# First keys and queries in fp32 through the sync queue, rounded on VectorE and ScalarE, in a hard-max attention kernel

## The chip, the cores and the metric

The kernel runs on one core of a Trainium2 chip. The metric is the device time of one execution in microseconds (us). The kernel before took 443.18 us (median of three runs, 442.71 to 443.21). The profile shown here is of one execution, whose span from first to last instruction is 441.9 us.

## The reference

For each of 4 batches there are 4096 queries and 4096 keys of 128 numbers. Each query gets the row of `v` that belongs to its best key:

```python
logits = np.matmul(q, k.transpose(0, 2, 1))      # 4 x 4096 x 4096
best = np.argmax(logits, axis=-1)
return v[b_idx, best, :]                          # 4 x 4096 x 128, fp32
```

## The kernel before

A tile is 128 queries; there are 32 tiles per batch and 128 in all. For each tile, TensorE (PE) screens all 4096 keys of the batch in fp16, not one by one but in groups of four. The transposed keys `kT` hold sums and differences of key pairs. `dpart` (line 228) multiplies a query tile with the differences, and ScalarE (ACT) takes the absolute value of the 1024 results into `A` (line 234). `spart` multiplies with the sums, and adds `A` on PE through an identity matrix. ACT turns one half into `E` (line 247), VectorE (DVE) takes the maximum of `E` and the other half into `W` (line 260, `fold`), and `max` reads the eight best groups of `W` (line 264, `top`). So a tile needs three ACT passes (two `A`, one `E`) and two long DVE passes, and PE keeps four PSUM buffers (pool `ps`, tag `u`) in turn.

Behind this screen, GpSimd (POOL) gathers the key group of each winner by indirect DMA (`kg`, line 282), DVE forms the fp16 dot products and picks one of four keys (lines 300 to 333), and POOL gathers the rows of `v` (`vr`, line 342), which SyncE (SP) writes out. Rows whose result is too close to call are collected twice, halfway and at the end, and are worked out again in fp32; the tiles `FQ`, `FK`, `FV` and `FR` belong to that, and are set to zero at the start.

All five engines are under a hand-written order: each engine executes its instructions in the order in which the program text issues them, and a queue (SP's and POOL's also) is held up by the first instruction that waits.

The change touches the start, before the first tile. There the order is this.

- Lines 105 and 106: POOL issues DMAs which read fp32 keys and queries of batch 0 and write them as fp16: the first half of the keys (`natk[0]`, half 0, 512 KB written) and query tiles 0 to 3 (`natq[0]`). After the identity matrix (lines 115 and 116) it issues the second half in two pieces, query tiles 4 to 7 and query tiles 8 to 31. Then come POOL's constants: three `W` iotas (line 131), small iotas, `ones`, `tri` (line 161), and the zero fills (lines 171 and 172). After these POOL issues the key loads of batch 1 (line 66).
- Lines 108 to 113: DVE clears `wz`, and PE runs 14 matmuls on it, into two of the four PSUM buffers.
- Lines 665 to 679: `trn_half(u, h, ms, put)` makes one quarter `u` of `kT` for key half `h`. Eight matmuls with an identity (or its negative, `identn`) transpose and add or subtract key pairs; a copy out of PSUM, by ACT (`by_act`, line 190) or DVE (`by_dve`, line 193), follows. Half 0 of the keys is done first, then query tiles 0 to 3 (`trn_q`, line 214), then half 1 in two steps, `ms` (0, 1) and (2, 3), one for each piece. Then the first `dpart` can run.
- `put_k` (line 75) subtracts keys within groups on DVE into `kd`, and SP stores them to DRAM for the later gathers (line 78). `turn_q` (line 208) has SP issue a DMA that transposes query tiles: tiles 4 to 7 first, then 8 to 15 and so on. Tile 4 needs the first of these. SP's order before is: store of `put_k(0, 0)`, transposes of tiles 4 to 7 and 8 to 15, store of `put_k(0, 1)`, two more transposes.

Of the kernel before, what the change touches and what calls it, by code (L numbers as in the profile page):

```python
# [7 lines left out]
FP32 = mybir.dt.float32  # L8
# [8 lines left out]
AF = mybir.ActivationFunctionType  # L17
# [12 lines left out]
def kernel(ctx, tc, q, k, v, out):  # L30
    nc = tc.nc
    B, Sq, D = q.shape
    Sk = k.shape[1]
    P = 128
    NQT = Sq // P
# [10 lines left out]
    bp = ctx.enter_context(tc.tile_pool(name="kq", bufs=1))  # L46
# [13 lines left out]
    natk = [bp.tile([P, 2, 16, P], FP16, name=f"natk{i}", tag=f"natk{i}") for i in range(2)]  # L60
    kd = bp.tile([P, 2, 4, 3, P], FP16, name="kd", tag="kd")
    natq = [bp.tile([P, NQT, P], FP16, name=f"natq{i}", tag=f"natq{i}") for i in range(2)]

    def load_k(b, h, x, y):
        kb = k[b].rearrange("(h p n) d -> p h n d", p=P, n=16)
        nc.gpsimd.dma_start(out=natk[b % 2][:, h, x:y], in_=kb[:, h, x:y])  # L66

    def load_q(b, x, y):
        nc.gpsimd.dma_start(out=natq[b % 2][:, x:y], in_=q[b].rearrange("(p t) d -> p t d", p=P)[:, x:y])  # L69

    def put_k(b, h):
        if b >= B:
            return
        src = natk[b % 2][:, h].rearrange("p (g f) d -> p g f d", f=4)
        nc.vector.tensor_tensor(out=kd[:, h], in0=src[:, :, 1:4, :], in1=src[:, :, 0:1, :].to_broadcast([P, 4, 3, P]),
                                op=OP.subtract)
        kb16 = k16[b].rearrange("(h p n) d -> p h (n d)", p=P, n=16)
        nc.sync.dma_start(out=kb16[:, h], in_=kd[:, h].rearrange("p g f d -> p (g f d)"))
# [23 lines left out]
        else:  # L102
            load_q(b, (i - 8) * NQT // 8, (i - 8 + n // 4) * NQT // 8)

    load_k(0, 0, 0, 16)
    load_q(0, 0, 4)

    wz = cp.tile([P, 512], FP16, tag="wz")
    nc.vector.memset(wz, 0.0)
# [4 lines left out]

    ident = cp.tile([P, P], FP32, tag="ident")
    masks.make_identity(nc, ident)
    load_k(0, 1, 0, 8)
    load_k(0, 1, 8, 16)
    load_q(0, 4, 8)
    load_q(0, 8, NQT)  # L120
    identh = cp.tile([P, P], FP16, tag="identh")
    nc.vector.tensor_copy(out=identh, in_=ident)
    identn = cp.tile([P, P], FP16, tag="identn")
# [6 lines left out]
    for W in W_t:  # L130
        nc.gpsimd.iota(out=W.bitcast(U16)[:, 0::2].rearrange("p (h m r) -> p h m r", h=2, m=4),
                       pattern=[[-NG * 2, 2], [-4, 4], [-16, P]], base=IDX, channel_multiplier=0)

    def iota(name, n, base, mult=0):
        x = cp.tile([P, n], FP32, name=name, tag=name)
        nc.gpsimd.iota(out=x, pattern=[[0 if mult else 1, n]], base=base, channel_multiplier=mult,
                       allow_small_or_imprecise_dtypes=True)
        return x
# [28 lines left out]
    FR = cp.tile([P, 8], U32, tag="FR")  # L167
    FQ = cp.tile([P, P], FP32, tag="FQ")
    FK = cp.tile([P, 3, 512], FP32, tag="FK")
    FV = cp.tile([P, P], FP32, tag="FV")  # L170
    for z in (FR, FQ, FK, FV):
        nc.gpsimd.memset(z, 0)

    tk_t = {}

    def trn_half(u, h, ms, put=None):
        x = 2 * (u // 2)
        if ms[0] == 0:
            tk_t[u] = pp.tile([P, 512], FP32, tag="u", name=f"tk_{u}_{h}")
        ps = tk_t[u]  # L180
        for m in ms:
            o = ps[:, m * P:(m + 1) * P]
            nc.tensor.matmul(out=o, lhsT=natk[0][:, h, 4 * m + x, :], rhs=identh, start=True, stop=False)
            nc.tensor.matmul(out=o, lhsT=natk[0][:, h, 4 * m + x + 1, :],
                             rhs=identn if u % 2 else identh, start=False, stop=True)
        if put is not None:
            put(kT[0][:, u * 1024 + h * 512:u * 1024 + h * 512 + 512], ps)

    def by_act(dst, src):
        nc.scalar.activation(out=dst, in_=src, func=AF.Copy)  # L190
# [20 lines left out]
    def trn_q(x, y, put):  # L211
        ps = pp.tile([P, 512], FP32, tag="u", name=f"tq_{x}")
        for i in range(x, y):
            nc.tensor.matmul(out=ps[:, (i - x) * P:(i - x + 1) * P], lhsT=natq[0][:, i, :], rhs=identh,
                             start=True, stop=True)
        put(qT[0][:, x * P:y * P], ps)
# [5 lines left out]
    def mm(ps, t, u, stop):  # L222
        b, qt = t // NQT, t % NQT
        for n in range(2):
            nc.tensor.matmul(out=ps[:, n * 512:(n + 1) * 512], lhsT=qT[b % 2][:, qt * P:(qt + 1) * P],  # L225
                             rhs=kT[b % 2][:, u * 1024 + n * 512:u * 1024 + (n + 1) * 512], start=True, stop=stop)

    def dpart(t, x):
        if t >= T:
            return  # L230
        ps = pp.tile([P, 1024], FP32, tag="u", name=f"pd_{t}_{x}")
        mm(ps, t, 1 + 2 * x, True)
        A = ep.tile([P, 1024], FP16, tag=f"A{x}", name=f"A_{t}_{x}")
        nc.scalar.activation(out=A, in_=ps, func=AF.Abs)  # L234
        A_t[t, x] = A
# [427 lines left out]
                nc.vector.tensor_scalar(out=base, in0=base, scalar1=float(Sk), scalar2=None, op0=OP.add)  # L663

    ALL = range(4)
    trn_half(1, 0, ALL, by_act)
    trn_half(3, 0, ALL, by_dve)
    trn_half(0, 0, ALL, by_act)
    trn_q(0, 4, by_dve)
    trn_half(2, 0, ALL, by_act)  # L670
    put_k(0, 0)
    for u in (1, 3, 0, 2):
        trn_half(u, 1, (0, 1))
    trn_half(1, 1, (2, 3), by_act)
# [2 lines left out]
    trn_half(2, 1, (2, 3), by_dve)  # L677
    dpart(0, 0)
    dpart(0, 1)
    nc.vector.tensor_copy(out=iota_h, in_=iota_r)  # L680
    nc.vector.tensor_copy(out=rec2[:, :, 1], in_=iota_p.to_broadcast([P, SLOTS]))
    cuts = list(range(0, 96 + 1, 8)) + list(range(96 + 4, T - 3, 4)) + [T - 2, T]
# [106 lines left out]
    for b in range(1, B):  # L789
        x = b * NQT  # L790
# [115 lines left out]
```

## Time and profile before

| engine | busy us | share of the span |
|---|---|---|
| DVE | 405.9 | 92% |
| PE | 378.9 | 86% |
| ACT | 375.6 | 85% |
| POOL | 306.2 | 69% |

A share of busy time is an average over the whole span. The stages differ:

| stage, us | ACT busy, us | DVE busy, us | POOL busy, us |
|---|---|---|---|
| 0 to 13 (loads, transposes of batch 0) | 3.71 | 4.11 | 11.78 |
| 13 to 40 (first tiles) | 27.00 | 20.26 | 8.53 |
| 40 to 110 | 70.00 | 69.28 | 43.50 |
| 110 to 220 | 109.54 | 110.00 | 81.68 |
| 220 to 330 | 101.33 | 109.72 | 83.03 |
| 330 to 425 | 64.03 | 90.90 | 69.71 |

The first stage is the only one before the tail in which neither ACT nor DVE is full.

### The profile page before, as it was taken

The numbers are of one execution on the slowest core, as the hardware profiler recorded it, in microseconds if no ns is written. First come the engines' busy times: TensorE is split into PE (matmuls) and PEld (weight loads), VectorE is DVE, ScalarE is ACT, GpSimd is POOL, SyncE is SP. The second block draws the span as 40 slices with busy tenths as digits, with TensorE's granted clock in tenths as the row PEclk, the third lists the DMA queues.
The fourth block names the chain that finished last, engine by engine and source line by source line (L and its number), as shares of the span: only waits on it lengthen the run. The fifth ranks groups of instructions, "written<-read, shape, count | busy, mean of one in ns | idle before, by whom it ended". The sixth has DMA issues, their size and how long they took to land.

```text
span 441.9 us, 6163 instructions
## 1 busy us (share of the span) xinstructions
PE 378.9 (86%) x1830; PEld 168.0 (38%) x1830; DVE 405.9 (92%) x734; ACT 375.6 (85%) x437; POOL 306.2 (69%) x335
## 2 busy tenths in 40 slices
PE   7999999999999999999998889999889997892100
PEld 4444444444444444444443334443333333330100
DVE  2688999999999999999999999999999999999840
ACT  2899999999999999999998889999989998892000
POOL 8413456677768786777777776777777777777673
PEclk9999999999999999999999999999999999998555
DMA  7933999463326999743336993453322332323432
GB/s 123 202 101 65 157 148 139 106 130 80 108 58 134 180 163 170 147 114 91 84 94 142 173 162 100 96 132 107 85 82 84 90 89 80 88 80 102 122 113 53
DMA packets 52868, 50.54 MB, mean 114 GB/s; under 512 B 34136, under 2 KB 40890, under 8 KB 52832
## 3 DMA queue, kind: packets, MB, share of 16 engines
q0 software_dynamic: 19072, 33.87, 39.2%
q1 hardware_dynamic: 33760, 16.26, 14.5%
q8 instruction: 14, 0.23, 0.2%
q14 instruction: 22, 0.18, 0.2%
HBM read 40.05 MB, written 14.55 MB: 124 GB/s over the span
## 4 chain that ended last, share of the span: by engine, by line
ACT 37%; issue 20%; DVE 13%; PE 12%; POOL 8%; DMA 8%; POOLq 0%; ACTq 0%; DVEq 0%; SPq 0%
ACT A L234 31%; ACT E L247 6%; DVE TOP L264 4%; PE psn L225 4%; POOL vr L342 4%; PE pd L225 4%; POOL kg L282 4%; DVE W L260 4%; PE psn L244 3%; DMA vr<-in_v_dram,win 3%; DMA natk<-in_k_dram 2%; DMA out_dram<-vr 1%; DMA kg<-k,cand 1%; DVE prod L300 1%; DMA vr<-in_v_dram,win_w 1%
## 5 line engine op out<-in xcount | busy, mean ns | idle before, releaser
L234 ACT ACTIVATE A<-pd 128x1024 f16<-128x1024 f32 x256 | 260.8, 1046 | 12.5 <-PE pd L225 12.0
L282 POOL DMA_INDIRECT kg<-k,cand x126 | 126.4, 1003 | 80.0 <-DVE cand L276 48.7
L260 DVE SCALAR_TENSOR_TENSOR W<-psn,E 128x1024 int16<-128x1024 f32 x128 | 167.1, 1306 | 7.4 <-ACT E L247 5.3
L225 PE MATMUL psn<-kT,qT 128*128 128x512 f16 x512 | 151.9, 378 | 11.4 <-ACT A L234 4.0
L225 PE MATMUL pd<-kT,qT 128*128 128x512 f16 x512 | 151.9, 379 | 8.7 <-ACT A L234 8.2
L264 DVE MAX8 TOP<-W 128x8 f32<-128x1024 f32 x128 | 157.0, 1227 | 0.0
L225 PEld LDWEIGHTS <-qT 128*128 128x128 f16 x1024 | 97.9, 97 | 151.8 <-issue 62.0
L342 POOL DMA_INDIRECT vr<-in_v_dram,win x126 | 125.9, 999 | 40.0 <-issue 36.1
L244 PE MATMUL psn<-A,identh 128*128 128x512 f16 x512 | 152.1, 378 | 0.0
L247 ACT ACTIVATE E<-psn 128x1024 int16<-128x1024 f32 x128 | 132.6, 1036 | 2.3 <-PE psn L244 1.5
L244 PEld LDWEIGHTS <-identh 128*128 128x128 f16 x512 | 49.6, 97 | 60.7
L300 DVE TENSOR_TENSOR prod<-kg,natq 128x768 f16<-128x768 f16 x63 | 34.8, 554 | 0.4 <-DMA kg<-k,cand 0.4
L205 ACT ACTIVATE kT<-uk 128x256 f16<-128x256 f32 x48 | 20.6, 429 | 1.5 <-PE uk L202 1.5
L305 DVE TENSOR_TENSOR p<-prod 128x768 f16<-128x768 f16 (+1 forms) x36 | 18.1, 502 | 0.1
L310 DVE TENSOR_REDUCE D<-p 128x12 f32<-128x384 f16 (+1 forms) x36 | 17.7, 492 | 0.1
L201 PE MATMUL uk<-identh,natk 128*128 128x128 f16 x96 | 15.8, 218 | 0.0
L484 PE MATMUL fp_e<-n_e,tri 128*128 128x1 f32 x2 | 0.6, 364 | 13.5 <-DVE n_e L482 13.5
L202 PEld LDWEIGHTS <-natk 128*128 128x128 f16 x96 | 9.3, 97 | 7.2 <-issue 5.1
L308 DVE TENSOR_TENSOR p<-p 128x384 f16<-128x384 f16 (+1 forms) x36 | 11.9, 330 | 0.1
L66 POOL DMA_DIRECT2D natk<-in_k_dram x19 | 11.3, 599 | 0.8 <-POOLq L890 0.8
L201 PEld LDWEIGHTS <-natk 128*128 128x128 f16 x96 | 9.3, 98 | 5.6
L69 POOL DMA_DIRECT2D natq<-in_q_dram x15 | 9.2, 614 | 0.0
(152 smaller groups left out, 140.1 us busy)
## 6 DMA issues: line engine op xcount, KB each, us to landing
out_dram<-vr SPq DMA_DIRECT2D x31, 256.0 KB, 2.1
natq<-in_q_dram POOLq DMA_DIRECT2D x12, 256.0 KB, 5.3
natk<-in_k_dram POOLq DMA_DIRECT2D x10, 256.0 KB, 4.5
k<-kd SPq DMA_DIRECT2D x18, 128.0 KB, 3.7
k<-natk POOLq DMA_DIRECT2D x6, 384.0 KB, 6.4
kg<-k,cand POOLq DMA_INDIRECT x126, 3.0
vr<-in_v_dram,win POOLq DMA_INDIRECT x126, 2.7
natk<-in_k_dram POOLq DMA_DIRECT2D x8, 128.0 KB, 5.7
```

Of the source, the lines that this page charges most:

```text
L201: nc.tensor.matmul(out=o, lhsT=natk[b % 2][:, h, 4 * m + x, :], rhs=identh, start=True, stop=False)
L205: nc.scalar.activation(out=kT[b % 2][:, c:c + 256], in_=ps, func=AF.Copy)
L225: nc.tensor.matmul(out=ps[:, n * 512:(n + 1) * 512], lhsT=qT[b % 2][:, qt * P:(qt + 1) * P], rhs=kT[b % 2][:, u * 1024 + n * 512:u * 1024 ...
L234: nc.scalar.activation(out=A, in_=ps, func=AF.Abs)
L244: nc.tensor.matmul(out=ps[:, n * 512:(n + 1) * 512], lhsT=identh, rhs=A[:, n * 512:(n + 1) * 512], start=False, stop=True)
L247: nc.scalar.activation(out=E, in_=ps, func=AF.Relu, scale=QSCALE)
L260: nc.vector.scalar_tensor_tensor(out=W_t[t % NW].bitcast(I16)[:, 1::2], in0=ps, scalar=QSCALE, in1=E, op0=OP.mult, op1=OP.max)
L264: nc.vector.max(out=TOP[:, t, :], in_=W_t[t % NW].bitcast(FP32))
L282: near_q.append(lambda j=j: nc.gpsimd.indirect_dma_start(out=kg[:, j].rearrange("p f d -> p (f d)"), out_offset=None, in_=k16[t0 // NQT], ...
L300: nc.vector.tensor_tensor(out=prod[:, i:i + h], in0=kg[:, i:i + h], in1=natq[b % 2][:, x + i - b * NQT:x + i + h - b * NQT, :].unsqueeze(2 ...
L305: nc.vector.tensor_tensor(out=p1, in0=prod[:, :, :, 0:64], in1=prod[:, :, :, 64:128], op=OP.add)
L342: late_q.append(lambda j=j: nc.gpsimd.indirect_dma_start(out=vr[:, j, :], out_offset=None, in_=v_flat, in_offset=IOA(ap=win[:, i + j:i + j ...
```

## The change

The first 4096 keys of batch 0 and its query tiles 0 to 3 are no longer rounded by the DMA. SP loads them as fp32 into two new tiles, `wide_k` and `wide_q`, by five plain DMAs at the very start. DVE rounds the first key half (two casts of 128x1024), piece 0 of the second half (128x1024) and five eighths of the last piece (128x640); ACT rounds the queries (128x512) and the rest of the last piece (128x384). POOL no longer issues these loads. It makes the identity and the three `W` iotas first, then loads query tiles 4 to 7, then makes the other constants, and then loads query tiles 8 to 31. The zero fills of `FQ`, `FK` and `FV` are moved from POOL to ACT, as five copies of zeros from `wz`; they stand first in ACT's order. `put_k(0, 0)` is moved from before the second half of `kT` to behind the first two `dpart`.

```diff
-    load_k(0, 0, 0, 16)
-    load_q(0, 0, 4)
+    wide_k = bp.tile([P, 2, 16, P], FP32, tag="wide_k")
+    wide_q = bp.tile([P, 4, P], FP32, tag="wide_q")
+    first_k = k[0].rearrange("(h p n) d -> p h n d", p=P, n=16)
+    nc.sync.dma_start(out=wide_k[:, 0, 0:8], in_=first_k[:, 0, 0:8])
+    nc.sync.dma_start(out=wide_k[:, 0, 8:16], in_=first_k[:, 0, 8:16])
+    nc.sync.dma_start(out=wide_q, in_=q[0].rearrange("(p t) d -> p t d", p=P)[:, 0:4])
+    nc.sync.dma_start(out=wide_k[:, 1, 0:8], in_=first_k[:, 1, 0:8])
+    nc.sync.dma_start(out=wide_k[:, 1, 8:16], in_=first_k[:, 1, 8:16])
...
     masks.make_identity(nc, ident)
-    load_k(0, 1, 0, 8)
-    load_k(0, 1, 8, 16)
-    load_q(0, 4, 8)
-    load_q(0, 8, NQT)
...
     for W in W_t:
         nc.gpsimd.iota(...)
+
+    load_q(0, 4, 8)
...
-    for z in (FR, FQ, FK, FV):
-        nc.gpsimd.memset(z, 0)
+    nc.gpsimd.memset(FR, 0)
+    for z in (FK[:, 0], FK[:, 1], FK[:, 2], FQ, FV):
+        nc.scalar.activation(out=z, in_=wz[:, 0:z.shape[1]], func=AF.Copy)
+    load_q(0, 8, NQT)
...
     ALL = range(4)
+
+    def narrow(put, h, x, y):
+        put(natk[0][:, h, x:y], wide_k[:, h, x:y])
+
+    narrow(by_dve, 0, 0, 8)
+    narrow(by_dve, 0, 8, 16)
+    by_act(natq[0][:, 0:4], wide_q)
     trn_half(1, 0, ALL, by_act)
     trn_half(3, 0, ALL, by_dve)
     trn_half(0, 0, ALL, by_act)
+    narrow(by_dve, 1, 0, 8)
     trn_q(0, 4, by_dve)
     trn_half(2, 0, ALL, by_act)
-    put_k(0, 0)
+    narrow(by_dve, 1, 8, 13)
+    narrow(by_act, 1, 13, 16)
     for u in (1, 3, 0, 2):
         trn_half(u, 1, (0, 1))
...
     dpart(0, 0)
     dpart(0, 1)
+    put_k(0, 0)
```

## The prediction

> **What bounds the kernel now.** I read the stages first (busy time in given stretches), because the change lies in the first 13 us only. Columns: stretch, its length, then busy us of PE, PEld, DVE, ACT and POOL with instruction counts, granted clock, DMA share, GB/s.
>
> ```profile
> 0.00:13.00 13.00, 10.38 (x86) 5.99 (x87) 4.11 (x12) 3.71 (x6) 11.78 (x32) 1.00 0.82 139
> 13.00:40.00 27.00, 26.02 (x127) 11.57 (x126) 20.26 (x22) 27.00 (x32) 8.53 (x13) 1.00 0.68 128
> 40.00:110.00 70.00, 68.19 (x343) 30.94 (x341) 69.28 (x94) 70.00 (x87) 43.50 (x46) 1.00 0.69 121
> ```
>
> From 13 us ACT is never idle (27.00 of 27.00, 70.00 of 70.00), and later DVE isn't. So an us gained or lost before ACT's first `A` should move everything behind it by an us, and nothing else in the change can matter if it stays hidden behind ACT. The question is therefore: when does the first `A` start (12.96 us before), and can ACT then run without a gap? The chain that ended last, for the start, then the timeline by engine (start, duration, engine, line, what, and idle time before it with its releaser):
>
> ```profile
> 3.67 7.54 DMA natk<-in_k_dram
> 11.21 0.05 issue
> 11.26 0.23 PE tk L183
> ...
> 12.34 0.61 PE pd L225 x2
> 12.94 0.02 issue
> 12.96 1.03 ACT A L234
> ```
>
> ```profile
> 1.19 5.24 PE L113 MATMUL warm<-wz 128*128 128x512 f16 x14 [1.19 <-DVE wz L109]
> 6.65 0.23 PE L183 MATMUL tk<-identh,natk 128*128 128x128 f16 x1 [0.22 <-DMA natk<-in_k_dram]
> 9.94 0.23 PE L183 MATMUL tk<-identh,natk 128*128 128x128 f16 x1 [0.83 <-DMA natk<-in_k_dram]
> 11.26 0.23 PE L183 MATMUL tk<-identh,natk 128*128 128x128 f16 x1 [0.25 <-DMA natk<-in_k_dram]
> ```
>
> ```profile
> 3.19 0.23 DVE L122 CAST identh<-ident 128x128 f16<-128x128 f32 x1 [2.06 <-POOL ident masks.py:199]
> 7.76 0.69 DVE L193 CAST kT<-tk 128x512 f16<-128x512 f32 x1 [4.04 <-PE tk L184]
> 8.43 0.69 DVE L193 CAST qT<-tq 128x512 f16<-128x512 f32 x1
> 9.04 0.95 DVE L75 TENSOR_TENSOR kd<-natk 128x1536 f16<-128x1536 f16 x1
> 16.77 1.31 DVE L260 SCALAR_TENSOR_TENSOR W<-psn,E 128x1024 int16<-128x1024 f32 x1 [2.75 <-ACT E L247]
> ```
>
> ```profile
> 5.24 3.74 POOL L131 IOTA W<- 128x1024 uint16 x3
> 10.61 0.73 POOL L161 TENSOR_SCALAR tri<-iota_r,iota_p 128x128 f32<-128x128 f32 x1
> ```
>
> ```profile
> 10.01 0.35 SPq L78 DMA_DIRECT2D k<-kd  x1
> 11.86 6.10 SPq L208 DMA_TRANSPOSE qT<-natq  x2
> ```
>
> The last key piece (11.26) carries the first `A`; from there to `A` it is 12.96 - 11.26 = 1.70 us of PE, copies and `pd`. The first key half (6.65) comes only 0.22 us after PE's 14 warm matmuls: these end at 6.43, and PE can't start earlier than that however early keys land.
>
> [...] a 384 KB store of SP took 6.5 us and a four-tile transpose 6.9 us beside POOL's loads. [...]
>
> **Part by part.** I sum against the profiled span of 441.9 us and carry the difference over to the median of 443.18.
>
> Removed on POOL: four of its six first loads (the other two move back), and 1.37 + 0.19 + 0.19 us of zero fills. POOL is idle for 14.37 us before its first gather at 30.67, so this is worth nothing by itself. Added on ACT: three fills of 128x512 at 0.60 (as the copies of L190) and two short ones, about 2.3 us; ACT is idle from 2.01 to 7.31. Nothing.
>
> Landing of the fp32 loads. SP starts near 0.8 and issues each in 0.35 us (L78). SP's 256 KB output stores landed in 2.1 us (median). The last 512 KB of keys came in 11.26 - 9.94 = 1.32 us, 397 GB/s of fp32; at this rate the store's data take 0.66, so 1.4 us are fixed. First data by 2.2 us; then 1.05 MB of keys to 4.9, queries 5.5, next piece 6.8, last piece 8.2, or 8.8 with the 0.26 MB of tiles 4 to 7 between. The trace also has a slow stretch, 0.79 MB from 6.65 to 9.94, 239 GB/s: then the last piece lands at 2.2 + 2.36 MB / 239 = 12.1. I take the fast end[...].
>
> Casts on DVE. 1024 elements: [...] 0.69, some 0.60 from start to start; 640 elements 0.43. Key half 0 is cast by about 5.7, before PE is free at 6.43: a gain of 0.22 there. Then DVE is the chain. Copy of `tk` 7.76 - 0.22 = 7.54 to 8.17, cast to 8.77, `qT` copy to 9.40, last cast to 9.83. ACT: `tk` copies, the last near 8.9 to 9.5, then its 384 elements (0.39 for 256 and 0.60 for 512 in L205 and L190: 0.5) to 10.0. The query cast (0.60 from about 5.5) is over before ACT's first `tk` copy. So PE starts the last pieces near 9.95 instead of 11.26: a gain of 1.3.
>
> [...] Between nothing and about 0.9: the iotas of `W` (1.25 each) now run from about 1.5 to 5.2 or later, beside `identh`, `identn` and the first casts, and `tri` (0.73) may lie beside the cast at 8.17. If the first casts end at 7 instead of 5.7, PE starts 0.5 late; `tri` can add 0.4. I take 0.3: gain 1.0, first `A` at 11.95.
>
> `put_k(0, 0)` on DVE now comes after the copies of `kT`, 0.84 us after the first `A` (13.80 - 12.96 before), and ends 1.8 us after it. DVE idles 2.75 us before its first `W`, so 0.95 us is hidden. But behind it on SP wait the store and then the transpose of tiles 4 to 7. That transpose starts about 2.2 us after the first `A` instead of 1.1 us before it. PE took tile 4 at 21.75, 8.8 us after the first `A`, with another 0.5 of room (its 0.59 us ended before ACT's turn at 22.93). The transpose took 6.9 us: landing 9.1 after the first `A`, against 9.3. With 8.75 from the store's issue to that landing, as before, it is 10.6: a stall of 1.3. By then POOL's loads are equally thick (tiles 8 to 31, then batch 1). I take 0.1, and keep 0 to 1.3. Tiles 8 to 15 are needed 11 us later than tile 4: hidden. The batch 1 loads of POOL start earlier, and their first use on PE is at 27.25: hidden.
>
> Sum: 1.3 - 0.3 - 0.1 = 0.9 to 1.0 gained; 443.18 - 1.0 = 442.2.
>
> **Rivals.**
> 1. [...] 0.9 lost of 1.3, gain 0.4, 442.8. For it: the W iotas are put right beside the casts. [...]
> 2. The wait for tile 4 takes the place of the wait for keys: gain 1.0 to 1.3 less a stall of 1.3, 443.2 (to 443.5). For it: the 8.75 us above. Against: less other traffic toward the end of it.
> 3. Slower: SP's fp32 loads run at the slow rate. The last piece lands at 12.1, its cast ends at 12.6, PE starts at 12.7 instead of 11.26: 1.4 lost, 444.6. It decides from a landing later than about 10.75, that is below 2.36 MB / (10.75 - 2.2) = 276 GB/s.
> 4. The gain at the start doesn't reach the end, since a later wait (POOL's gathers, the out stores near 236 us) takes it: 443.2.
>
> **How the numbers follow.** Chances: forecast 0.46 (its own range 441.7 to 442.6), [...] tile 4 stall 0.14, slow loads 0.12, absorbed 0.06. A measurement of this kernel tells 0.2%, 0.9 us, from no change. The forecast lies nearly wholly beyond it, [...] the two at 443.2 nearly wholly within: faster 0.46, same 0.40, slower 0.14 (the slow loads and a large stall). From 441.4 to 443.9 leaves out most of the slow loads and a little on the low side; the gain can't pass 1.35 or so, as PE's warm matmuls and DVE's chain stand against it.
>
> **What would show it.** Right: first `tk` at 6.4 to 6.6, the last pieces on PE near 10, first `A` near 11.9, no ACT gap near its ninth `A`, and every later stretch shifted alike. Casts of 1024 longer than 0.7 us, or idle DVE before them with POOL named or busy, mean rival 1. ACT idle before tile 4's first `A`, with PE waiting for the `qT` transpose, means rival 2. Casts of DVE that wait for a load past 10 us mean rival 3. Equal first `A` gain but an equal end means rival 4. I am wrong altogether if a later stage, after 40 us, changes its length by more than 0.5 us.

## The result, and the profile after

The changed kernel took 448.29 us (median of four runs, 447.49 to 449.70) against 443.10 for the kernel before: a ratio of 1.0122, with a 95% interval of 1.0096 to 1.0148. I had forecast 442.2. The profiled run was the fastest of the four (447.49); its span is 445.7 us against 441.9. Eight of the later experiment runs fell on chips that granted TensorE about 0.9 of its clock and took about 530 us with every kernel; of these only the first 30 us and the end are read, and no time.

The stages first, with the columns of the prediction (stretch, its length, busy us of PE, PEld, DVE, ACT and POOL with instruction counts, granted clock, DMA share, GB/s).

```profile
0.00:13.00 13.00, 10.15 (x88) 6.12 (x89) 7.46 (x16) 7.29 (x13) 11.73 (x31) 1.00 0.82 227
13.00:40.00 27.00, 24.25 (x117) 10.73 (x116) 20.44 (x21) 25.62 (x31) 5.24 (x6) 1.00 0.71 130
40.00:110.00 70.00, 68.19 (x345) 31.06 (x343) 68.48 (x93) 70.00 (x87) 42.74 (x45) 1.00 0.67 120
```

In the second stage ACT is no longer full: 25.62 of 27.00. The timeline of DVE, ACT, PE and SP says when and why.

```profile
1.35 1.29 DVE L124 CAST identh<-ident 128x128 f16<-128x128 f32 x1 [0.21 <-POOL ident masks.py:199]
4.64 0.98 DVE L199 CAST natk<-wide_k 128x1024 f16<-128x1024 f32 x1 [1.77 <-DMA wide_k<-in_k_dram]
6.07 0.69 DVE L199 CAST natk<-wide_k 128x1024 f16<-128x1024 f32 x1 [0.45 <-DMA wide_k<-in_k_dram]
8.98 0.69 DVE L199 CAST natk<-wide_k 128x1024 f16<-128x1024 f32 x1 [0.59 <-DMA wide_k<-in_k_dram]
```

```profile
10.23 0.52 ACT L196 ACTIVATE natk<-wide_k 128x384 f16<-128x384 f32 x1 [0.81 <-DMA wide_k<-in_k_dram]
...
12.49 2.85 ACT L240 ACTIVATE A<-pd 128x1024 f16<-128x1024 f32 x3 [0.68 <-PE pd L231]
...
24.05 1.02 ACT L240 ACTIVATE A<-pd 128x1024 f16<-128x1024 f32 x1 [1.38 <-PE pd L231]
```

```profile
23.35 0.61 PE L231 MATMUL pd<-kT,qT 128*128 128x512 f16 x2 [1.92 <-DMA qT<-natq]
```

```profile
14.21 0.33 SPq L78 DMA_DIRECT2D k<-kd  x1
14.58 4.26 SPq L214 DMA_TRANSPOSE qT<-natq  x2
```

The first `A` starts at 12.49, 0.47 earlier than before. Then, before tile 4, PE waits 1.92 us for the transposed queries, whose DMA SP issued only at 14.58, behind the store. Following the maximum of each tile (`top`) through both timelines gives the shift against the kernel before: -0.47 us at tile 0, +1.00 at tile 6, +1.01 at tile 66, +0.76 at tile 127. So the start costs about 1 us, and between tile 6 and tile 84 nothing changes. From tile 110 to 120 b_merge4, b_pool4 and b_sp5 (below), which have nothing of the change, gain 0.5 us too on this one trace of the kernel before, so the fall to +0.76 is not the change's.

That isn't 5 us, nor the 3.8 us of the two spans. The last link of the chain is nearly at the same time in both (437.53 after, 437.46 before). So 0.7 us more of the start's loss had gone by there in this run, and what is left lies behind that link, at the program's end. These are SP's own waits there (waited for, us in total, times, longest), first after, then before:

```profile
SPq L917 <- PEq L917: 4.6, 2, 4.0
SPq L917 <- DMA out_dram<-FV,rowk_e: 3.4, 1, 3.4
```

```profile
SPq L901 <- DMA out_dram<-FV,rowk_e: 3.6, 1, 3.6
...
SPq L901 <- PEq L901: 0.7, 2, 0.5
```

The profile, by its inference, puts SP's longest wait at the end (4.0 us) down to PE. The instructions of that line (engine, operation, times, shortest, median and longest in ns, then the start of the first and of the last) show that PE has little to do with it:

```profile
L917 POOLq DRAIN  x3: 46/109/7340, 437.5 to 445.4; - x3
...
L917 PEldq DRAIN  x2: 8/8/8, 422.8 to 445.2; - x2
```

```profile
L901 POOLq DRAIN  x3: 46/109/3253, 437.5 to 441.6; - x3
```

POOL's long drain, an instruction at the very end of its queue, is the first of the three: it takes 7.34 us instead of 3.25, from the same start at 437.5. That is 4.1 us of the loss. It goes on for 4.9 us after SP's wait for the last output is over (440.0). What follows it takes 0.8 us instead of 1.2, which is why the spans differ by only 3.8.

### The profile page after: what moved, and what is told of

It reads as the page before. It is cut to its first block, busy times and chain, and to the rows that moved or that the text cites. A ratio compares the mean times of both kernels' runs of the same rounds, so it can differ in the third digit from the quotient of the medians.

```text
span 445.7 us, 6172 instructions
## 1 busy us (share of the span) xinstructions
PE 377.5 (85%) x1830; PEld 167.9 (38%) x1830; DVE 409.7 (92%) x738; ACT 377.9 (85%) x444; POOL 303.0 (68%) x328
## 4 chain that ended last, share of the span: by engine, by line
ACT 37%; DVE 20%; issue 19%; PE 13%; DMA 7%; POOL 1%; POOLq 0%; SPq 0%; ACTq 0%; DVEq 0%
ACT A L240 31%; DVE TOP L270 7%; ACT E L253 6%; DVE W L266 5%; PE pd L231 4%; PE psn L231 4%; PE psn L250 4%; DMA qT<-natq 2%; DVE prod L306 2%; DMA wide_k<-in_k_dram 2%; DMA vr<-in_v_dram,win 1%; DVE p L311 1%; DMA kg<-k,cand 1%; DMA FK<-in_k_dram,gb_e 1%; DVE p L314 1%
## 5 line engine op out<-in xcount | busy, mean ns | idle before, releaser
L240 ACT ACTIVATE A<-pd 128x1024 f16<-128x1024 f32 x256 | 260.2, 1042 | 15.2 <-PE pd L231 15.0
L66 POOL DMA_DIRECT2D natk<-in_k_dram x16 | 9.4, 598 | 0.0
```

## The experiments

Theory A: the drain depends on how many DMAs POOL has issued; the change took four away (309 before, 305 after, summed over the rows of POOL's DMAs). Rivals: B, SP's five new loads; C, something else in the program. For tile 4, theory 1: the transpose is late because it stands behind the store. Its rival: POOL's traffic makes it slow in any place. In the labels, a and b are the changed kernel and the kernel before; t and q build on a_turn1st.

**a_turn1st.** The transpose goes ahead of the store.

```diff
+    turn_q(0, 4, 8)
     dpart(0, 0)
     dpart(0, 1)
     put_k(0, 0)
...
-        if it == 1:
-            turn_q(0, 4, 8)
```

> The changed kernel with one move: SP issues the transpose of query tiles 4 to 7 before the store of the first half of the key differences instead of behind it. Theory 1 (the transpose stands behind the store, which waits for the late kd): PE's wait for the qT transpose before tile 4 (1.92 us in the changed kernel) goes to 0, ACT runs without a gap, and the ninth maximum is 1.0 to 1.5 us earlier than in the changed kernel, about 0.4 us earlier than in the kernel before. Rival (the transpose is slow because of POOL's loads of tiles 8 to 31 and of batch 1, whatever stands in front of it): the wait stays above 1 us. The time after the last work (POOL's last wait for itself, 7.3 us in the changed kernel against 3.3 before) is not touched by this: it should stay near 7, so the whole gains 1.0 to 1.5 us at most.

Measured: 446.12 us (445.98 to 446.45), ratio 1.0064 (1.0048 to 1.0081). SP's queue:

```profile
10.86 1.36 SPq L214 DMA_TRANSPOSE qT<-natq  x1
14.28 0.33 SPq L78 DMA_DIRECT2D k<-kd  x1
```

PE has no wait for `qT` left and the shift is -0.42 at tile 6 and -0.64 at tile 127. Theory 1 holds. (The medians of the two kernels lie 2.2 us apart, more than these 1.4 us; a likely reason follows with a_pool4.) POOL's drain is 7.34 us still; t_split5 below shows that without it this kernel is no slower than before.

**a_pool4, b_pool4, b_sp5.** Extra loads in the middle of tile 12, four on POOL or five on SP:

```diff
+        if it == 12:
+            for x, n in ((0, 16), (0, 4), (0, 8), (8, 8)):
+                nc.gpsimd.dma_start(out=spare[:, 0:n], in_=...)
```

> The changed kernel, with four more loads on POOL in the middle of tile 12, of the sizes of the four that the change took from POOL, into a tile that nothing reads. Theory A (POOL's last drain depends on how many DMAs, or how many of their descriptors, POOL issued before): with the number of before restored the drain falls from 7.3 us to about 3.3 and the kernel gains about 4 us. Rival B (the five loads of SP lengthen the end): the drain stays near 7.3. Rival C (neither, some other difference of the program): stays near 7.3, too.

> The kernel before with the same four extra loads on POOL in the middle of tile 12. Theory A: POOL's last drain changes from 3.3 us, the size and sign open, several us possible. Rivals B and C: it stays near 3.3 and the time stays within 0.5 us of the kernel before.

> The kernel before with five extra fp32 loads of SP in the middle of tile 12, of the sizes of the five that the change added, into a tile that nothing reads. Rival B (SP's five loads lengthen the end): POOL's last drain grows from 3.3 us to about 7 and the time by about 4 us. Theory A and rival C: it stays near 3.3 us, and the time within 0.5 us of the kernel before.

Measured drains: 3.25 (a_pool4, 309 DMAs), 3.34 (b_pool4, 313), 3.25 (b_sp5, 309). The times (457.91, 454.41 and 447.52) can't be used: the extra loads of POOL write one tile and so wait for each other, 15.4 us in a_pool4 and 15.2 in b_pool4, and the gathers queue behind them; in b_sp5 a POOL transfer of batch 1's keys waited 12.6 us for SP's stores. That was a fault of my design. The drains stand: restoring the number brings the short one back, and SP's loads don't make a long one. B falls.

a_pool4 starts like the changed kernel, but here PE's wait for tile 4 was 2.98 us, and PE's matmuls then came at half the pace; what decides on that is read with a_split5 (the columns are start and duration; two of 128x512 each):

```profile
24.42 0.60 PE L233 MATMUL pd<-kT,qT 128*128 128x512 f16 x2 [2.98 <-DMA qT<-natq]
24.86 0.71 PE L233 MATMUL psn<-kT,qT 128*128 128x512 f16 x2
25.37 1.06 PE L252 MATMUL psn<-A,identh 128*128 128x512 f16 x2
26.22 1.06 PE L233 MATMUL pd<-kT,qT 128*128 128x512 f16 x2
27.07 1.06 PE L233 MATMUL psn<-kT,qT 128*128 128x512 f16 x2
27.93 0.94 PE L252 MATMUL psn<-A,identh 128*128 128x512 f16 x2
28.70 0.59 PE L233 MATMUL pd<-kT,qT 128*128 128x512 f16 x2
```

Pairs stand 0.85 us apart instead of 0.43 until about 28, and the shift at tile 6 is 3.59 us instead of 1.00. So one and the same start of the program can lose 1.0 or 3.6 us. That may be why the other runs of the changed kernel were up to 2.2 us slower than the profiled one; they left no trace, so it isn't shown.

**t_split5, t_split3, b_merge4.** Now the number of DMAs alone; the bytes that they move stay the same. The first two are a_turn1st with one load cut up; the third is the kernel before with loads merged.

```diff
-    load_q(0, 8, NQT)
+    for x, y in ((8, 12), (12, 16), (16, 20), (20, 24), (24, NQT)):
+        load_q(0, x, y)
```

```diff
         if it < 8:
-            load_part(1, it, 4)
+            if it % 2 == 0:
+                load_part(1, it)
```

> The version with the early transpose (tiles 4 to 7 transposed before the store), and POOL's one load of query tiles 8 to 31 cut into five, so that POOL issues 309 DMAs as in the kernel before, with the same bytes as in the changed kernel. Theory A (POOL's last drain depends on the number of DMAs or descriptors that POOL issued): the drain falls from 7.3 us to 3.3, and the whole to about 442.3 us, 0.5 to 1 us below the kernel before. Rival C (the drain depends on something else in the program, and the extra loads of the last experiment touched it by chance): 7.3 us and about 446.

> The same with the load cut into three, so 307 DMAs of POOL. Theory A, if the drain steps at some number between 305 and 309, gives either 3.3 us or 7.3, and tells on which side of 307 the step lies; if it grows with each missing DMA by about 1 us, it gives about 5.3. Rival C: 7.3.

> The kernel before, with the eight first key loads of batch 1 merged into four of twice the size, so that POOL issues 305 DMAs, as many as in the changed kernel; SP's loads, the casts and the zero fills are as before. Theory A: POOL's last drain grows from 3.3 us to about 7.3, and the kernel takes about 447 us without any other part of the change. Rival C: the drain stays at 3.3 and the time within 0.5 us of the kernel before.

Measured: t_split5 (309 DMAs) 442.34 us, ratio 0.9978 (0.9971 to 0.9985). t_split3 (307) 446.55, 1.0078 (1.0061 to 1.0095). b_merge4 (305) 447.30, 1.0092 (1.0076 to 1.0109). The instructions of the last line, in this order:

```profile
L917 POOLq DRAIN  x3: 46/109/3253, 436.5 to 440.3; - x3
```

```profile
L917 POOLq DRAIN  x3: 46/109/7503, 436.9 to 445.0; - x3
```

```profile
L902 POOLq DRAIN  x3: 46/109/7335, 437.5 to 445.4; - x3
```

b_merge4 settles it: it has nothing of the change, its tiles lie between 0.5 us earlier and 0.05 us later than those of the kernel before (tile 127 is 0.47 earlier), and it still takes 4.1 us longer. Theory A holds, with a step and not a slope: 307 is no better than 305. And t_split5 beats the kernel before.

**t_split4, t_split17, b_merge1, b_merge2.** Where the step lies. The first two are a_turn1st with the load cut into 4 and 17; the other two are the kernel before with two or four of batch 1's loads merged into one or two.

> The version with the early transpose and POOL's load of tiles 8 to 31 in four pieces: 308 DMAs of POOL. If the drain has a threshold in the number of DMAs between 307 (7.5 us) and 309 (3.3 us), this shows on which side 308 lies: 3.3 or 7.3 us, nothing between. No theory says which.

> The same in seventeen pieces: 321 DMAs of POOL, 16 more than the changed kernel's 305. If the long drain comes back with every 16 DMAs, it is 7.3 us here; if there is a threshold between 307 and 309 and nothing more, 3.3 us. The small pieces cost POOL some 8 us at the start and may delay the tiles themselves; only the drain is to be read.

> The kernel before with two of batch 1's first key loads merged into one, so 308 DMAs of POOL. If the long drain has its threshold in the number of POOL's DMAs between 307 and 308, whatever else the kernel does: 3.3 us and no change in time (442.7 to 443.7). If what counts is not the number: could be either.

> The kernel before with four of these loads merged into two, so 307 DMAs of POOL: drain about 7.3 us and 447 us if the threshold in the number holds also without the change; 3.3 us and 443 if not.

Measured drains: 3.26 us (t_split4, 308 DMAs), 3.79 (t_split17, 321), 3.26 (b_merge1, 308), 7.50 (b_merge2, 307). The first and the last two:

```profile
L917 POOLq DRAIN  x3: 46/109/3257, 518.6 to 522.4; - x3
```

```profile
L901 POOLq DRAIN  x3: 46/109/3257, 522.4 to 526.7; - x3
```

```profile
L901 POOLq DRAIN  x3: 46/109/7503, 530.7 to 538.7; - x3
```

In both kernels the step is between 307 and 308, and it doesn't come back at 321. In the traces each load that POOL issues more or less changes the packets of its queue by 144, whatever its bytes (18,784 with 307 DMAs, 18,928 with 308, in both kernels). So the bytes are out, but whether DMAs or their packets are counted stays open, and so does what POOL does in those 4 us.

**a_split5 and its repetitions.** The changed kernel with only the five-piece load, to time the wait for tile 4 by itself.

> The changed kernel with only one thing added: POOL's load of query tiles 8 to 31 cut into five, so that POOL issues 309 DMAs. Theory A: the drain is 3.3 us, and the time falls from 448.3 by about 4.1 to 444.2, which leaves the wait before tile 4 (1 to 3 us, differing from run to run) as the only loss: slower than the kernel before by 0.5 to 1.5 us. Rival C: 448.

> The changed kernel with POOL's load of tiles 8 to 31 cut into five, once more, on another chip. Theory A: drain 3.3 us, time 444 to 445 (about 4.1 below the changed kernel), what is left above the kernel before being the wait for tile 4. Rival C: 448.

> The changed kernel with 309 DMAs of POOL, for its time on an unthrottled chip. The long drain gone and the wait for tile 4 left (1.9 to 3.9 us on PE in its profiles so far): 444 to 446, above the kernel before and 3 to 4.5 us below the changed kernel. If 448, then the drain is not what the time paid for.

Measured (a_split5_c): 447.21 us, ratio 1.0095 (1.0068 to 1.0121), a miss: I had said 444 to 446. The drain is short (3.25 us), but the wait for tile 4 is worse than with the load in one piece: 3.40, 3.89 and 3.65 us in the three profiles (a_split5, a_split5_r, a_split5_c). ACT's gap in a_split5_c:

```profile
26.25 1.02 ACT L241 ACTIVATE A<-pd 128x1024 f16<-128x1024 f32 x1 [3.54 <-PE pd L232]
```

PE was again at half pace after it, and the shift is +4.24 at tile 6 and +3.93 at tile 127. So the time is accounted for, but the cut took 4.1 us from the end and added about 3 at the start. Why the transpose is slower beside five loads than beside one isn't settled.

The length of the wait alone doesn't decide on the half pace. The longest, in a_split5_r, left the pace as it was:

```profile
25.38 0.60 PE L232 MATMUL pd<-kT,qT 128*128 128x512 f16 x2 [3.89 <-DMA qT<-natq]
25.82 0.59 PE L232 MATMUL psn<-kT,qT 128*128 128x512 f16 x2
26.25 0.59 PE L251 MATMUL psn<-A,identh 128*128 128x512 f16 x2
```

In the traces PE's granted clock changes only on a grid of 3.41 us, which lies elsewhere in each run. In the kernel before and in the changed one it stays at full for 399.4 us, 117 such steps, up to 404.72 and up to 403.68. These are windows of that grid around the wait, with the columns of the stages (PE's busy time comes after the length, the granted clock is third from the end): two of a_pool4, then three of a_split5_r.

```profile
21.79:25.21 3.42, 0.79 (x4) 0.41 (x5) 2.41 (x2) 0.99 (x2) 0.00 (x0) 1.00 1.24 175
25.21:28.62 3.41, 3.41 (x10) 1.18 (x8) 0.00 (x0) 2.87 (x3) 0.00 (x0) 0.50 0.79 184
```

```profile
19.95:23.36 3.41, 1.54 (x7) 0.48 (x5) 3.08 (x4) 2.78 (x4) 0.00 (x0) 1.00 1.24 211
23.36:26.78 3.42, 1.40 (x7) 0.70 (x8) 0.89 (x1) 0.70 (x1) 0.00 (x0) 1.00 1.26 230
26.78:30.19 3.41, 3.41 (x18) 1.52 (x17) 1.96 (x2) 3.41 (x5) 0.00 (x0) 1.00 0.58 129
```

In a_pool4 the wait fills most of one window, and the next has half the clock; in a_split5_c a whole window without work (21.61 to 25.02) stands before it. In a_split5_r the wait falls on two windows, PE works 1.54 and 1.40 us in them, and the clock stays. Over twelve profiles (both kernels, a_turn1st, a_pool4, b_pool4, b_sp5, t_split5, t_split3, b_merge4, t_qlate, a_split5_c, q_split5_c) every window at full clock in which PE was busy for 37% or less was followed by one at half, and every one with 44% or more by one at full. In the profile of the changed kernel PE was busy for 1.50 of 3.42 us from 21.39 (44%), and full clock followed; it was busy for 0.87 of 3.42 from 400.26 (25%), and half followed. The half pace costs about 1.5 us, an estimate from two runs: from tile 0 to tile 6 a_split5_c falls back by 4.69 us with a wait of 3.65, a_split5_r by 3.45 with its longer wait of 3.89.

**t_qlate, q_split5 and its repetitions.** POOL's load of tiles 4 to 7 is moved behind the constants, first with the long drain, then with five pieces.

```diff
-    load_q(0, 4, 8)
...
     nc.gpsimd.memset(FR, 0)
+    load_q(0, 4, 8)
```

> The version with the early transpose, with POOL's load of query tiles 4 to 7 moved from behind the W iotas to behind the constants, so that it doesn't run beside SP's fp32 loads. If the DMA engines' sharing delayed the last key piece (which came near 10.2 us instead of my 8.2 to 8.8), the first A starts up to 0.7 us earlier than the 12.55 us of that version; if SP's loads are slow by themselves, by less than 0.2. The transpose of tiles 4 to 7 moves back too, by about 3 us, and may bring its wait before tile 4 back. The drain stays near 7.3.

> All mendings together: the changed kernel with the transpose of tiles 4 to 7 before the store, POOL's load of tiles 4 to 7 behind the constants, and 309 DMAs of POOL. First A near 12.3 us, drain 3.3 us; 442.0 to 442.4, 0.8 to 1.2 us below the kernel before, and the same or up to 0.3 us below the version whose load of tiles 4 to 7 is early. If the later transpose makes PE wait again before tile 4, it is 442.5 or more.

> All mendings together, once more, on another chip: first A near 12.25 us as before; 442.0 to 442.4 if PE doesn't wait for tile 4, 442.5 to 443.2 if it waits by about 1 us as it did in the last run (1.1 us).

> All mendings together, on an unthrottled chip: 442.0 to 442.6, first A at 12.3 to 13.0 us and a wait before tile 4 of 0.3 to 1.1 us, as in its two profiles so far.

Measured: in t_qlate the first `A` is at 12.29, against 12.55 in a_turn1st. But kernels with the same order up to there differ by as much: a_turn1st and the four t_split kernels lie between 12.55 and 12.81, and the four with the late load at 12.25, 12.29, 12.35 and 12.97. So a gain from not sharing the DMA engines isn't shown. The loads are slow without this neighbour too: in those four the wait for the last key piece ended between 9.9 and 10.7 us, where I had 8.2. t_qlate took 446.14 us (1.0081, 1.0064 to 1.0097), with the drain at 7.34. q_split5_c took 442.72, ratio 0.9981 (0.9971 to 0.9991); PE waits 0.86 us for `qT` again, which takes back most of what the earlier start gave (1.1 and 0.3 us in its two other profiles). It is no better than t_split5.

The ratios to the kernel before, by the two causes:

| | long drain (305 DMAs) | short drain (309 DMAs) |
|---|---|---|
| wait before tile 4 | changed kernel 1.0122 | a_split5_c 1.0095 |
| no wait | a_turn1st 1.0064 | t_split5 0.9978 |

That t_split5's 442.34 comes so near to my forecast of 442.2 is partly luck. Its first `A` is only 0.37 us earlier than in the kernel before, and so are its tiles up to tile 84; the rest of its 0.9 us comes later, and some 0.3 us of that b_merge4, which has nothing of the change, gains as well.

## Why the prediction was wrong, point by point

- **Where the start sets the time.** Right. The shift of 1.0 us at tile 6 is still 1.0 at tile 84, and -0.42 in a_turn1st is still -0.47.
- **Removed on POOL.** This is the step that failed. I priced four DMAs less at nothing, because POOL idles 14 us before its first gather. At the place they were taken from, they are worth nothing. But their number sets POOL's drain at the very end: 7.34 us against 3.25, shown by b_merge4 without any of the change. No view of the kernel before named this; its drain of 3.25 us was within the last 4.4 us of the span that I didn't open. My closing sentence, that I would be wrong altogether if a later stage changed its length, looked in the right direction, but none of my rivals did.
- **The transpose behind the store.** The mechanism was there, the size was wrong. I took a stall of 0.1 us and kept 1.3 as the end of the range; the move from -0.47 to +1.00 is 1.47. Of my two ways to the landing, the one from the store's issue was right: the transpose was issued 2.09 us after the first `A` (predicted 2.2), and PE got it 10.86 after it (predicted 10.6; the other way gave 9.1). I had no term for PE's clock: in a_pool4 and a_split5_c, where the wait filled most of one of the 3.41 us windows, the half clock after it cost another 1.5 us, by the estimate from a_split5_c and a_split5_r.
- **Landing of the fp32 loads.** Mis-sized. The end of the wait for each load on DVE or ACT was 6.07 us for the first key half (predicted 4.9), 8.98 for the next piece (6.8), and 10.23 for the last (8.2 to 8.8). The 2.62 MB, from 2.2 us on, came at 328 GB/s, between my two ends of 397 and 239; I had taken the fast one, by a guess. In a_turn1st the chain that ended last runs through the first piece of the second key half, which landed at 9.03, and its cast: loads, and not a queue of casts on DVE as I had it, set the time. PE's warm matmuls, which I took to hold PE until 6.43 us, ended at 5.91: PE's clock was at full 1.05 us earlier in this run (from 4.31 instead of 5.36; the warm matmuls began every 0.43 us before that and every 0.22 after it). With the loads this late it made no difference.
- **Casts.** Right in price: 0.69 us for 1024 elements as forecast, and 0.49 instead of 0.43 for 640. The forecast was an estimate of mine: no view of the kernel before shows a cast from fp32 in SBUF of either size.
- **DVE beside POOL's iotas.** Right that DVE can be slower there, wrong in the cost. The trace of the kernel before didn't show it: its `identh` took 0.23 us and was over before the first `W` iota (5.24). The 0.3 us that I took off, and the 0.22 that I gave to rival 1, were my estimate. After the change, `identh`, begun 0.07 us after the first `W` iota, took 1.29 us and ended 0.08 us after it, and the first cast, begun at 4.64 while the third iota ran (to 5.08), took 0.98 instead of 0.69. What holds DVE up there isn't shown. But the next cast waited for its load anyway (0.45), so the 0.3 us were not paid.
- **Sum.** The first `A`: forecast 11.95, measured 12.49, a gain of 0.47 instead of 1.0. Then -1.47 for tile 4, and -4.1 for the drain: a loss of 5.1, near the 5.2 between the medians. That agreement is partly chance, for in the profiled run itself 0.9 of the start's 1.0 us had gone by the last link of the chain, and its span is only 3.8 us longer.

## What to carry to other kernels

Before calling DMAs on an idle engine free to add or drop, look at the last microseconds of the span too: read which engine's drain ends last there, and compare it when the number of that engine's DMAs changes. When work is moved back on an engine, write down what its results wait for in a queue behind them; here a store that nobody needed soon held up a transpose that everybody did. With both mended, the change gives 0.2%.

## What the runs showed of the hardware that I had not expected

- POOL's drain at the end took 7.3 to 7.5 us in every kernel here with 305 or 307 DMAs of POOL (six profiles), and 3.25 to 3.8 us in every one with 308 to 321.
- PE's granted clock changed on a grid of 3.41 us in these traces, and it fell to half also after windows in which PE was not idle: windows with PE busy for up to 37% (1.27 of 3.41 us in t_split5, from 398.47) were followed by half clock. So where a wait fell on the grid counted here, and not its length alone: 2.98 us in a_pool4 was followed by half clock, 3.89 us in a_split5_r was not.
- The same start (changed kernel and a_pool4) gave a wait of 1.92 us in one profile and of 2.98 in another.
